# A two-layer hybrid trunk on one core: the first quarter of the first MLP matrix becomes seven block products

## The chip, the cores and the metric

The kernel runs on one core of one Trainium2 chip. The metric is the device time of one execution in microseconds. Three runs of the kernel before the change took 1278.21, 1278.3 and 1280.88 us, so its median is 1278.3 us. One more execution was profiled.

## The reference

Two layers. Each normalises its input, runs a mixer (windowed attention beside an mLSTM, gated and projected), and then a squared-ReLU MLP. The change touches the MLP alone:

```
for layer in range(2):
    x = mixer(x, ...)
    u = relu(rmsnorm(x, norm_ffn) @ w_ff1)      # x: 512 tokens x 1024, w_ff1: 1024 x 4096
    x = x + (u * u) @ w_ff2                     # w_ff2: 4096 x 1024
```

All values are float32. `setup_inputs` draws normal inputs and weights and scales five of the small gains.

## The kernel before, in words

**Three products for one.** TensorE is fed float32r operands. For the precision of float32, each operand is split into a high part (ScalarE copies it to float32r, L1212) and a low part (VectorE subtracts the high part from the original, L1213); `mm3` then issues high x high, high x low and low x high (L47). So each weight block of 128 partitions x 1024 costs one ScalarE and one VectorE operation before TensorE may use it. The weights' parts lie in a pool of four buffers each (`spl`).

**Quarters.** `mlp` (one call per layer) cuts the 4096 hidden columns into four quarters of 1024. The first matrix makes a quarter of u, feature-major; the second matrix adds that quarter's contribution to the tokens in `xtok`. A quarter of either matrix is a product of 2 x 2 blocks: the first matrix has blocks of 512 inputs by 512 columns, against two halves of the inputs (rows j = 0, 1) and two halves of 256 tokens.

**Seven block products.** `first_slots` (for quarters 1 to 3 before the change) and `second_slots` (for all four) compute the 2 x 2 block product with seven block products, numbered 1 to 7, instead of eight, from sums and differences of blocks. A product of the first matrix is called fQ.n here, one of the second pQ.n, with Q the quarter. Each is a `Slot` of two halves: `prep` loads and splits the weights of a half, `run` issues its matmuls, `done` reads the result from PSUM, and `acts_` prepares the second matrix's other operand (`u_split`). fQ.n has 48 matmuls of 256 columns, pQ.n 24 matmuls of 512 columns.

Sums of weight blocks are made by transfers from GpSimd's queue that accumulate (`more`, L1382 and L1560) or by VectorE (`plus`, L1249). Sums of the normalised inputs (t1 to t4) are made once per layer by VectorE in `t_steps`; each is then split by `two_parts`. For the results, `first_read` copies a product from PSUM, `then_read` (L1478 to L1480) adds a second one to it by VectorE and runs ReLU and square on ScalarE, and `only_read` does ReLU and square straight from PSUM.

**The first quarter before the change** is not done so. `First` computes 256 of its columns with 8 x 2 x 3 matmuls of 512 columns. Two of them run at once, step by step over the eight input tiles, in the order 4 to 7 and then 0 to 3. While they do the first four, the input tiles 0 to 3 are still being finished: the steps in `late` transpose each (L52), split it (L180, L181) and sum its squares (L262), and `factor` makes the row factors. Two further `First` follow as slots.

**The order of the work.** The list `slots` writes the order on TensorE by hand:

```
f01 (two First together), First 2, First 3,
p0.1 f1.1 p0.2 f1.2 p0.5 f1.5 p0.6 f1.6 p0.3 f1.7 p0.7 f1.4 p0.4 f1.3,
(the same for quarters 1/2 and 2/3, the last one ending ... p2.7 f3.4 p2.4 f3.3),
p3.1 p3.5 p3.2 p3.6 p3.3 p3.7 p3.4
```

When half i starts, `go` first issues the weights of all halves up to i + 3, then the operand of the next slot, then the matmuls of half i; at the end of a slot `done`, then what `extra` holds for that half (t1 to t4). Each engine runs its instructions strictly in the order that the framework's scheduler gives them; `high_priority` moves splits, sums and PSUM reads forward in it. Weight loads go out on SP's queue (`ask`, L1239) into eleven buffers (`raw`) that lie on memory of the mixer; the first four loads of an MLP are chained in their order, the others are not.

**A dependency that counts below.** p3.5's operand is u(1,1) - u(1,0) of quarter 3, and u(1,0) is finished by product 3 of the first matrix (f3.3). So f3.3's read, ReLU, square, the difference, and its two parts lie between f3.3 and p3.5.

Of the kernel before, what the change touches and what calls it, by code (L numbers as in the profile page):

```python
# [33 lines left out]
def hybrid_kernel(ctx, tc, x, norm_mix, w_in, att_q_norm, att_k_norm, att_sinks, m_gate_bias,  # L34
# [53 lines left out]
    def banks(which):  # L88

        return now["psum"].tile([P, 2, T], F32, tag=which, name=nm("mm"))  # L90
# [1095 lines left out]
    def mlp(l, norm, late, phase):  # L1186
# [87 lines left out]
        class First:  # L1274


            def __init__(self, q, which="f"):
                self.q, self.which, self.w = q, which, {}

            def load(self, h):  # L1280
                with tc.high_priority():
                    r = raw([P, 4, H])
                    ask(r, w_ff1[l, 4 * h * P:4 * (h + 1) * P, H * self.q:H * (self.q + 1)]
                        .rearrange("(k p) n -> p k n", p=P))
                self.w[h] = w_split(r)
                drop(r)

            def step(self, k, order=range(KT)):
                if k == order[0]:
                    self.ps = banks(self.which)  # L1290
                hi, lo = self.w[k // 4]
                for m in range(2):
                    c = slice(m * P, (m + 1) * P)
                    mm3(self.ps[:, m, :], hi[:, k % 4, c], lo[:, k % 4, c], acts[k][0], acts[k][1],
                        k == order[0], k == order[-1])

            def evac(self, u):
                i, m = self.q // 2, 2 * (self.q % 2)
                with tc.high_priority():
                    for t in range(2):  # L1300
                        dst = u[t, i][:, m:m + 2, :]
                        sc.activation(dst, self.ps[:, :, H * t:H * (t + 1)], AF.Relu)
                        sc.activation(dst, dst, AF.Square)

# [5 lines left out]

        def first_slot(q, u, which):
            f = First(q, which)
            return Slot(f.load, lambda h: [f.step(k) for k in range(4 * h, 4 * h + 4)], lambda: f.evac(u))

# [10 lines left out]
        def t_steps():  # L1325

            (h11, l11), (h12, l12), (h21, l21), (h22, l22) = ([f32(a) for a in quad(j, t)]
                                                              for j in range(2) for t in range(2))

            def b12():  # L1330
                scratch["a"] = raw([P, 4, H])
                ve.tensor_tensor(scratch["a"], h12, l12, op=ALU.add)

            def t1():
                d = scratch["b"] = raw([P, 4, H])
                ve.tensor_tensor(d, h11, scratch["a"], op=ALU.subtract)
                ve.tensor_tensor(d, d, l11, op=ALU.add)
                t_parts[1] = two_parts(d, *t_new("t1"))

            def t2():  # L1340
                d = scratch["b"]
                ve.scalar_tensor_tensor(d, d, -1.0, h22, op0=ALU.mult, op1=ALU.subtract)
                ve.tensor_tensor(d, d, l22, op=ALU.subtract)
                t_parts[2] = two_parts(d, *t_new("t2"))

            def t3():

                d = scratch["a"]
                ve.tensor_tensor(d, h22, d, op=ALU.subtract)
                ve.tensor_tensor(d, d, l22, op=ALU.add)  # L1350
                t_parts[3] = two_parts(d, *quad(0, 1))
                drop(d)

            def t4():
                d = scratch["b"]
                ve.scalar_tensor_tensor(d, d, -1.0, h21, op0=ALU.mult, op1=ALU.subtract)
                ve.tensor_tensor(d, d, l21, op=ALU.subtract)
                t_parts[4] = two_parts(d, *t_new("t4"))
                drop(d)

            return [b12, t1, t2, t3, t4]

        def first_slots(part, new):
# [20 lines left out]
            def w2(h):  # L1384
                load(a12, h, 0, 1)
                return a12[h], lambda: None, a12[h]

            def w1(h):
                load(a11, h, 0, 0)

                def then():
                    load(s, h, 1, 0)
                    more(s, h, 1, 1)

                return a11[h], then, a11[h]
# [18 lines left out]
            def w4(h):  # L1414
                load(a22, h, 1, 1)
                return a22[h], lambda: None, a22[h]

            def fresh_y():
                ys[:] = [aux(), aux()]
# [3 lines left out]
            def product_(y, fresh, w, moving, done):  # L1423
# [9 lines left out]
                def run(h):  # L1433
                    if h == 0 and fresh:
                        if y:
                            fresh_y()
                        else:
                            pairs["f"] = banks("f")
# [55 lines left out]
            return {  # L1494
                1: product_(False, True, w1, lambda: quad(0, 0), done1),
                2: product_(True, not seeded, w2, lambda: quad(1, 0), done2),
                5: product_(True, True, w5, lambda: t_parts[1], lambda: first_read((1, 1), True, -1.0)),
                6: product_(False, False, w6, lambda: t_parts[2], lambda: first_read((1, 0), False)),
                7: product_(False, False, w7, lambda: t_parts[3], lambda: then_read((1, 1), False, ALU.subtract)),
                4: product_(False, False, w4, lambda: t_parts[4], lambda: only_read((0, 1), False, -1.0)),  # L1500
                3: product_(True, False, w3, lambda: quad(1, 1), lambda: then_read((1, 0), True, ALU.add)),
# [41 lines left out]
        def second_slots(part, u):  # L1543
# [28 lines left out]
            def w1(h):  # L1572
# [4 lines left out]
                load(qa, h, 0, 0)  # L1577
                load(b12, h, 0, 1)
# [33 lines left out]
            def s4():  # L1612
# [26 lines left out]
        f01, turned = [First(0, "f"), First(1, "y")], [4, 5, 6, 7, 0, 1, 2, 3]  # L1639
        for h in (1, 0):  # L1640
            for f in f01:
                f.load(h)
        weave([(0.5, lambda k=k, f=f: f.step(k, turned)) for k in turned for f in f01], late + [(4.5, factor)])
        for f in f01:
            f.evac(us[0])
        slots = [first_slot(2, us[0], "x"), first_slot(3, us[0], "f")]
        for part in range(4):
            p = second_slots(part, us[part])
            if part < 3:
                f = first_slots(part + 1, us[part + 1])  # L1650
# [99 lines left out]
```

## Time and profile before

| | |
|---|---|
| median of three runs | 1278.3 us (1278.21 to 1280.88) |
| profiled execution | 1280.18 us, span 1278.5 us |
| mean granted TensorE clock over the span | 0.999 |
| first matmul of the MLP, first and second layer | 317.8 and 953.5 us |
| HBM read | 188.95 MB |

The span runs from the first to the last instruction on the core; all times inside an execution are counted from its start. An engine's row gives when an instruction began and how long it took; matmuls overlap, so the pace of TensorE is the distance from one start to the next, not a matmul's own duration. A bracket behind a row is the time for which the engine had stood idle and what ended it. In the waits, the three numbers are the total in us, how often, and the longest.

### The profile page before, as it was taken

The numbers are of one execution on the slowest core, as the hardware profiler recorded it, in microseconds if no ns is written. First come the engines' busy times: TensorE is split into PE (matmuls) and PEld (weight loads), VectorE is DVE, ScalarE is ACT, GpSimd is POOL, SyncE is SP. The second block draws the span as 40 slices with busy tenths as digits, with TensorE's granted clock in tenths as the row PEclk, the third lists the DMA queues.
The fourth block names the chain that finished last, engine by engine and source line by source line (L and its number), as shares of the span: only waits on it lengthen the run. The fifth ranks groups of instructions, "written<-read, shape, count | busy, mean of one in ns | idle before, by whom it ended". The sixth has DMA issues, their size and how long they took to land.

```text
span 1278.5 us, 19222 instructions
## 1 busy us (share of the span) xinstructions
PE 1266.4 (99%) x6882; PEld 1090.9 (85%) x6882; DVE 1011.8 (79%) x1604; ACT 795.5 (62%) x1415; POOL 265.5 (21%) x361
## 2 busy tenths in 40 slices
PE   9999999999999999999999999999999999999998
PEld 7887888888889999998888888788888899999987
DVE  4788988688777787877857989876878777869787
ACT  5578578546565665656454885776466556566563
POOL 4514131030003031131115132310300030311300
PEclk9999999999999999999999999999999999999999
DMA  5425463476679789897224345534857798997953
GB/s 158 112 76 148 110 121 100 138 146 150 185 198 187 209 179 219 211 182 189 35 76 115 99 116 117 114 111 130 157 134 201 192 183 230 168 231 179 206 140 99
DMA packets 138928, 193.35 MB, mean 151 GB/s; under 512 B 10568, under 2 KB 79024, under 8 KB 138832
## 3 DMA queue, kind: packets, MB, share of 16 engines
q1 hardware_dynamic: 92992, 129.72, 33.1%
q0 software_dynamic: 45120, 62.00, 30.2%
q8 instruction: 54, 0.88, 0.3%
q10 hardware_dynamic: 720, 0.40, 0.1%
q14 instruction: 42, 0.34, 0.1%
HBM read 188.95 MB, written 2.10 MB: 149 GB/s over the span
## 4 chain that ended last, share of the span: by engine, by line
PE 88%; DVE 6%; ACT 3%; DMA 1%; POOL 1%; issue 1%; SPq 0%; DVEq 0%; ACTq 0%; POOLq 0%
PE mm L47 74%; PE aux L47 12%; PE aux L52 2%; DMA w<-in_w_in_dram 1%; ACT t L664 1%; DVE wl L168 1%; DVE wl L1213 1%; ACT wh L167 0%; DVE p L748 0%; DVE t L304 0%; DVE tq L625 0%; DMA w<-in_w_m_branch_dram 0%; POOL rp L547 0%; POOL rq L548 0%; DVE m L658 0%
## 5 line engine op out<-in xcount | busy, mean ns | idle before, releaser
L47 PE MATMUL mm<-i,wh 128*128 128x512 f32 (+1 forms) x1280 | 353.2, 363 | 0.0
L1213 DVE TENSOR_TENSOR wl<-raw,wh 128x1024 fp32r<-128x1024 f32 x212 | 257.1, 1222 | 116.1 <-ACT wh L1212 111.4
L1212 ACT ACTIVATE wh<-raw 128x1024 fp32r<-128x1024 f32 x212 | 222.8, 1054 | 172.6 <-PE mm L47 99.7
L47 PEld LDWEIGHTS mm<-i,wh 128*128 128x128 f32 x1280 | 221.8, 189 | 29.5
L47 PE MATMUL mm<-i,wl 128*128 128x512 f32 (+1 forms) x640 | 229.2, 359 | 0.0
L47 PE MATMUL mm<-wh,ul 128*128 128x512 f32 x440 | 172.1, 391 | 3.2 <-DVE ul L1213 3.2
L47 PE MATMUL mm<-wh,uh 128*128 128x512 f32 x440 | 172.7, 393 | 0.9 <-ACT uh L1212 0.9
L47 PE MATMUL mm<-wl,uh 128*128 128x512 f32 x440 | 172.3, 392 | 0.0
L1382 POOL DMA_DIRECT2D raw<-in_w_ff_dram x48 | 61.9, 1311 | 413.3 <-DVE wl L1213 222.9
L47 PEld LDWEIGHTS mm<-i,wl 128*128 128x128 f32 x640 | 120.9, 189 | 18.6
L167 ACT ACTIVATE wh<-w 128x512 fp32r<-128x512 f32 (+1 forms) x144 | 86.4, 603 | 61.6 <-PE mm L47 41.9
L168 DVE TENSOR_TENSOR wl<-w,wh 128x512 fp32r<-128x512 f32 (+1 forms) x144 | 96.4, 672 | 35.5 <-ACT wh L167 33.1
L47 PEld LDWEIGHTS mm<-wh,ul 128*128 128x128 f32 x440 | 83.0, 189 | 21.7 <-DVE ul L1213 4.0
L47 PE MATMUL mm<-wh,i 128*128 128x512 f32 (+1 forms) x352 | 99.8, 357 | 1.0 <-ACT wh L167 1.0
L47 PEld LDWEIGHTS mm<-wh,uh 128*128 128x128 f32 x440 | 83.1, 189 | 17.6 <-ACT uh L1212 1.7
L47 PEld LDWEIGHTS mm<-wl,uh 128*128 128x128 f32 x440 | 83.2, 189 | 15.7
L1267 DVE SCALAR_TENSOR_TENSOR x<-mm,ms,x 128x512 f32<-128x512 f32 x98 | 68.9, 745 | 10.7 <-PE mm L47 10.7
L1560 POOL DMA_DIRECT2D raw<-in_w_ff_dram x36 | 43.6, 1212 | 133.6 <-DVE wl L1213 100.9
L47 PEld LDWEIGHTS mm<-wh,i 128*128 128x128 f32 x352 | 62.0, 188 | 10.2 <-ACT wh L167 1.6
L47 PE MATMUL aux<-i,wh 128*128 128x256 f32 x384 | 69.5, 283 | 0.0
L47 PE MATMUL mm<-t,wh 128*128 128x256 f32 x384 | 69.5, 283 | 0.0
L47 PE MATMUL mm<-wl,i 128*128 128x512 f32 (+1 forms) x176 | 62.0, 352 | 0.2 <-DVE wl L168 0.2
(327 smaller groups left out, 2525.5 us busy)
## 6 DMA issues: line engine op xcount, KB each, us to landing
raw<-in_w_ff_dram SPq DMA_DIRECT2D x144, 512.0 KB, 5.1
raw<-in_w_ff_dram POOLq DMA_DIRECT2D x84, 512.0 KB, 8.5
w<-in_w_in_dram SPq DMA_DIRECT2D x112, 256.0 KB, 2.7
a<-in_w_in_dram POOLq DMA_DIRECT2D x32, 256.0 KB, 5.7
qa<-in_w_out_dram POOLq DMA_DIRECT2D x12, 512.0 KB, 5.8
a<-in_w_in_dram SPq DMA_DIRECT2D x16, 256.0 KB, 4.7
w<-in_w_att_branch_dram SPq DMA_DIRECT2D x16, 256.0 KB, 2.9
w<-in_w_m_branch_dram SPq DMA_DIRECT2D x16, 256.0 KB, 2.9
```

The lines of the kernel that those rows point to most:

```text
L47: latest[0] = nc.tensor.matmul(*args, **kw)
L52: latest[0] = nc.tensor.transpose(*args)
L167: sc.activation(wh[:, :off], raw[:, :off], AF.Copy)
L168: ve.tensor_tensor(wl[:, :off], raw[:, :off], f32(wh[:, :off]), op=ALU.subtract)
L664: sc.activation(s3[:, i, :], s3[:, i, :], AF.Exp, bias=m[:, i:i + 1], accum_out=den[:, i:i + 1])
L1212: sc.activation(hi, src, AF.Copy)
L1213: ve.tensor_tensor(lo, src, f32(hi), op=ALU.subtract)
L1267: ve.scalar_tensor_tensor(xh[:, cc], ps[i][:, cc], ms[j][:, b:b + 1], xh[:, cc], op0=ALU.mult, op1=ALU.add)
L1382: gp.dma_start(to[h], src(h, i, j), accum_op=ALU.add)
L1560: gp.dma_start(to[h], src(h, i, j), accum_op=ALU.add)
```

## The change

The class `First` and its slots are gone. Quarter 0 of the first matrix becomes f0.1 to f0.7, made by `first_slots(0, ...)`, for both layers. TensorE's order becomes

```
f0.2 f1.2 f0.1 f0.5 p0.1 f0.6 f0.7 f0.4 f0.3
f1.1 p0.5 f1.5 p0.6 f1.6 p0.3 f1.7 p0.7 f1.3 p0.4 f1.4 p0.2,
p1.1 f2.1 p1.2 f2.2 p1.5 f2.5 p1.6 f2.6 p1.3 f2.7 p1.7 f2.3 p1.4 f2.4,
(the same with quarters 2 and 3, ending ... p2.7 f3.3 p2.4 f3.4),
p3.1 p3.5 p3.2 p3.6 p3.3 p3.7 p3.4
```

so that products 3 and 4 of the first matrix have changed places everywhere. f0.2 and f1.2 use only inputs 4 to 7; the late inputs 0 to 3 are transposed and split between their halves. While a late input tile stands in PSUM, ScalarE also copies it whole (`turn_whole`, two copies of 128x256 per tile); t1, t2 and t3 are then made from the whole copies instead of from high and low parts. For quarter 0 the second block column of weights is summed by VectorE (`begin`) and then extended by accumulating transfers; p0.1's result is added to the tokens by itself (two operations of L1267) instead of being copied into p0.2's banks; and the weights of p0.5 are summed by a transfer instead of VectorE. The lines that carry this:

```diff
+        def turn_whole(k):
+            ps = norm.transposes(k)
+            norm.turn(k, ps)
+            if not whole:
+                whole[:] = [uspl.tile([P, 4, H], F32, tag="uh", name=nm("x")) for _ in range(2)]
+            for t in range(2):
+                sc.activation(whole[t][:, k, :], ps[:, H * t:H * (t + 1)], AF.Copy, scale=norm.gain(k))
+        def x22():
+            h22, l22 = [f32(a) for a in quad(1, 1)]
+            scratch["a"] = uspl.tile([P, 4, H], F32, tag="ul", name=nm("x"))
+            plus(scratch["a"], h22, l22)
+        def t1():
+            d = scratch["b"] = raw([P, 4, H])
+            plus(d, whole[0], whole[1], ALU.subtract)
+            with tc.high_priority():
                 t_parts[1] = two_parts(d, *t_new("t1"))
+        def t2():
+            d = scratch["b"]
+            neither(d, d, scratch["a"])
+            t_parts[2] = two_parts(d, *t_new("t2"))
+        def t3():
+            d = scratch["a"]
+            plus(d, d, whole[1], ALU.subtract)
+            t_parts[3] = two_parts(d, *quad(0, 1))
...
+            if part == 0:
+                def begin(h):
+                    load(c, h, 1, 0)
+                    load(s, h, 1, 1)
+                    plus(s[h], s[h], c[h])
+                    more(c, h, 0, 0)
+                def w2(h):
+                    load(a12, h, 0, 1)
+                    return a12[h], lambda: None, a12[h]
+                def w5(h):
+                    return s[h], lambda: more(s, h, 0, 0)
...
-                done1, done2 = lambda: first_read((0, 0), False), lambda: then_read((0, 0), True, ALU.add)
+                done1, done2 = lambda: then_read((0, 0), False, ALU.add), lambda: first_read((0, 0), True)
...
                 load(qa, h, 0, 0)
+                if part == 0:
+                    return qa[h], lambda: more(qa, h, 0, 1)
                 load(b12, h, 0, 1)
                 return qa[h], lambda: plus(qa[h], qa[h], b12[h]), b12[h]
...
+            alone = part == 0
-                1: product("x", True, w1, lambda: u[0, 0], [], "f" if end else "y"),
-                2: product("f" if end else "y", False, w2, lambda: u[0, 1], [(0, 0, end)]),
+                1: product("x", True, w1, lambda: u[0, 0], [(0, 0, False)] * alone,
+                           None if alone else "f" if end else "y"),
+                2: product("f" if end else "y", alone, w2, lambda: u[0, 1], [(0, 0, end)]),
...
+        begin0, f0 = first_slots(0, us[0], {2: "y", 5: "y"}, [lambda h: f1s[0](h)])
+        begin1, f1 = first_slots(1, us[1], {2: "x"}, [begin0])
+        slots = [f0[2], f1[2], f0[1], f0[5], p[1], f0[6], f0[7], f0[4], f0[3],
+                 f1[1], p[5], f1[5], p[6], f1[6], p[3], f1[7], p[7], f1[3], p[4], f1[4], p[2]]
+        for part in range(1, 4):
...
-                slots += [p[1], f[1], p[2], f[2], p[5], f[5], p[6], f[6], p[3], f[7], p[7], f[4], p[4], f[3]]
+                slots += [p[1], f[1], p[2], f[2], p[5], f[5], p[6], f[6], p[3], f[7], p[7], f[3], p[4], f[4]]
...
-        extra = dict(zip((1, 3, 7, 11, 15), t_steps()))
+        extra = {0: x22, 3: t1, 6: t2, 8: t3, 10: t4}
...
-        weave(steps, side)
+        weave([(1.0, go) for _, go in steps[:5]], norm.steps(0, 1.0, 0.5, turn_whole) + [(4.0, factor)])
+        weave(steps[5:], side)
```

More of the change, by code (lines that the diff above doesn't have):

```diff
@@ L1184, in mixer, with mlp @@
         return norm
-    def mlp(l, norm, late, phase):
+    def mlp(l, norm, phase):
         final = l == DEPTH - 1
@@ L1271, in gain @@
                                 out[0, b * P:(b + 1) * P, j * T + c[0]:j * T + c[1]], xh[:, cc])
[L1274 to L1303, printed above, removed]
         class Slot:
@@ L1323, in t_new @@
             return [comb.tile([P, 4, H], F32R, tag=f"{n}{p}", name=nm(n)) for p in "hl"]
[L1325 to L1337, printed above, removed]
-                t_parts[1] = two_parts(d, *t_new("t1"))
[L1340 to L1361, printed above, removed]
@@ L1363, in first_slots @@
-        def first_slots(part, new):
+        whole = []
+        def turn_whole(k):
[9 more added lines that the diff above has]
+            plus(scratch["a"], h22, l22)
@@ L1369, in first_slots, with t4 @@
+        def t4():
+            h21, l21 = [f32(a) for a in quad(1, 0)]
+            d = scratch["b"]
+            neither(d, d, h21)
+            plus(d, d, l21, ALU.subtract)
+            t_parts[4] = two_parts(d, *t_new("t4"))
+            drop(d)
+        def first_slots(part, new, places={}, begins=()):
             a11, a12, a22, s, c = ([None] * 2 for _ in range(5))
@@ L1385, in w2 @@
                 load(a12, h, 0, 1)
-                return a12[h], lambda: None, a12[h]
+                return a12[h], lambda: [f(h) for f in begins], a12[h]
+            def begin(h):
+                load(s, h, 1, 0)
+                more(s, h, 1, 1)
             def w1(h):
                 load(a11, h, 0, 0)
[L1391 to L1395, printed above, removed]
+                return a11[h], lambda: begin(h) if part > 1 else None, a11[h]
             def w5(h):
```

47 lines of the change are left out of this document (19 added, 28 removed).

## The prediction

> **What bounds the kernel.** First the page's busy times, then the waits of TensorE over the whole span.
>
> ```profile
> PE 1266.4 (99%) x6882; PEld 1090.9 (85%) x6882; DVE 1011.8 (79%) x1604; ACT 795.5 (62%) x1415; POOL 265.5 (21%) x361
> ```
>
> ```profile
> PE mm L47 <- DVE ul L1213: 3.2, 2, 1.6
> ...
> PE mm L47 <- ACT uh L1212: 0.9, 2, 0.4
> ```
>
> TensorE never rests for long, so the time changes only by the number and pace of its matmuls and by its few waits. The two rows are one wait at one place in each layer: for the parts of a second-matrix operand. The timeline of TensorE shows the place in the first layer.
>
> ```profile
> 598.14 0.28 PE L47 MATMUL aux<-i,wl 128*128 128x256 f32 x1
> ...
> 603.50 0.39 PE L47 MATMUL mm<-wh,ul 128*128 128x512 f32 x1
> 604.32 0.50 PE L47 MATMUL mm<-wh,uh 128*128 128x512 f32 x1 [0.43 <-ACT uh L1212]
> 604.65 0.40 PE L47 MATMUL mm<-wl,uh 128*128 128x512 f32 x1
> 606.63 0.67 PE L47 MATMUL mm<-wh,ul 128*128 128x512 f32 x1 [1.58 <-DVE ul L1213]
> ...
> 610.38 0.40 PE L47 MATMUL mm<-wh,ul 128*128 128x512 f32 x1
> ```
>
> 598.14 is the last matmul of f3.3, 603.50 the last of p3.1, 604.32 the first of p3.5. Then the clock: the column before the last two.
>
> ```profile
> 606.60:610.00 3.40, 3.37 (x8) 2.69 (x9) 3.38 (x3) 0.55 (x2) 0.00 (x0) 0.53 0.00 0
> ...
> 1243.00:1247.00 4.00, 4.00 (x20) 3.28 (x19) 3.65 (x4) 1.06 (x1) 0.00 (x0) 1.00 0.00 0
> ```
>
> After the wait of the first layer the granted clock was 0.53 and 3.4 us held only eight matmuls. After the equal wait of the second layer it stayed at 1.00.
>
> **Term 1, the matmuls.** The groups of the plain quarter (317.7 to 362.6 us), and the paces of a 512-column and a 256-column stream:
>
> ```profile
> L47 PE MATMUL mm<-i,wh 128*128 128x512 f32 x128 | 39.9, 393 | 0.0
> L47 PE MATMUL mm<-i,wl 128*128 128x512 f32 x64 | 25.0, 390 | 0.0
> ```
>
> ```profile
> 330.71 0.62 PE L47 MATMUL mm<-i,wh 128*128 128x512 f32 x2
> 331.16 0.39 PE L47 MATMUL mm<-i,wl 128*128 128x512 f32 x1
> 331.39 0.62 PE L47 MATMUL mm<-i,wh 128*128 128x512 f32 x2
> ```
>
> ```profile
> 369.18 0.40 PE L47 MATMUL mm<-i,wh 128*128 128x256 f32 x2
> 369.42 0.28 PE L47 MATMUL mm<-i,wl 128*128 128x256 f32 x1
> 369.54 0.40 PE L47 MATMUL mm<-i,wh 128*128 128x256 f32 x2
> ```
>
> Three matmuls take 0.68 us at 512 columns (0.227 each) and 0.36 us at 256 (0.12 each). The quarter now takes 192 x 0.227 = 43.5 us; seven products of 48 take 336 x 0.12 = 40.3 us. Saved 3.2 us a layer, **6.4 us** in all. An eighth less arithmetic gives only a fourteenth less time, since half a matmul costs more than half. The sixteen transposes stay. The Trainium skill ("TensorE: Matmul & The Clock Gate", Back-to-back issue gap) gives an isolated gap of N/2.4 + 2.5 ns, that is 216 and 109 ns; by it the saving would be an estimated 4.7 us a layer and the forecast below 1267.0. The measured paces, 227 and 120 ns, differ from it and decide.
>
> **Term 2, products 3 and 4 swapped.** From the rows of the timeline: 603.50 to 604.32 is 0.59 us over the pace, 604.32 to 604.65 is 0.11, 604.65 to 606.63 is 1.75, together 2.45 us in each layer; the eight slow matmuls cost another 3.40 - 8 x 0.227 = 1.6 us in the first layer. So 4.1 and 2.45 us. How the wait arises is on VectorE and ScalarE:
>
> ```profile
> 598.96 0.68 DVE L1478 TENSOR_TENSOR u<-u,aux 128x512 f32<-128x512 f32 x1
> ...
> 601.95 1.22 DVE L1249 TENSOR_TENSOR s<-u,u 128x1024 f32<-128x1024 f32 x1
> 603.08 1.22 DVE L1213 TENSOR_TENSOR wl<-raw,wh 128x1024 fp32r<-128x1024 f32 x1
> 604.22 1.22 DVE L1249 TENSOR_TENSOR u<-u,u 128x1024 f32<-128x1024 f32 x1
> 605.36 1.22 DVE L1213 TENSOR_TENSOR ul<-s,uh 128x1024 fp32r<-128x1024 f32 x1
> ```
>
> ```profile
> 599.67 1.06 ACT L1479 ACTIVATE u<-u 128x1024 f32<-128x1024 f32 x1 [0.27 <-DVE u L1478]
> 600.76 1.06 ACT L1480 ACTIVATE u<-u 128x1024 f32<-128x1024 f32 x1
> ...
> 603.20 1.06 ACT L1212 ACTIVATE uh<-s 128x1024 fp32r<-128x1024 f32 x1 [0.43 <-DVE s L1249]
> ```
>
> From f3.3's last matmul (ends 598.42) follow: sum, ReLU, square, difference, high part, ready at 604.26: 5.84 us. Only p3.1, 24 x 0.227 = 5.44 us, covers it. The low part is later still, for a weight split and the sum "u<-u,u" of the next slot run before it. With f3.3 moved in front of p2.4 and f3.4, the cover is p2.4, f3.4 and p3.1: 5.44 + 5.76 + 5.44 = 16.6 us for a chain that ended at 606.58, 8.2 us long. The wait goes: **6.5 us**. Late next there would be f3.4, whose result goes straight through ReLU and square into p3.2 with p3.1 and p3.5 as cover, 10.9 us against 1.06 x 3 + 1.22 = 4.4: nothing.
>
> **Term 3, the same chain anew.** In the new order f0.3, f1.1, p0.5 stand in a row. The chain is the one above (f0.3 finishes u(1,0), p0.5 needs the difference), its cover f1.1, 48 x 0.12 = 5.76 us instead of 5.44. p0.6's sum "u<-u,u" stands two slots behind p0.5 here, not one, so I take it out of the way; the weight split stays. High part 5.84 us after f0.3's end against about 5.6 due: 0.25. Low part one split end later, 1.2 us behind the high one, where 0.45 is free (it serves the third matmul): 0.75. So **1.0 us a layer, +2.0**; from 0 (a chain without its queueing: 0.68 + 1.06 + 1.06 + 1.22 + 1.06 = 5.1 us) to 4.1 (as before, with a slow clock).
>
> **Term 4, p0.1 behind f0.1.** Only f0.5 (5.76 us) lies between. Sum 1.22, ReLU, square and high part 1.06 each make 4.4 us, with the 0.75 us of queueing that the chain above had 5.2: in time. Low part 1.22 later, 6.4, against 5.6 + 0.45: 0.35 us a layer, **+0.7**; from 0 to 1.5 (one more split of 1.06 on ScalarE in front).
>
> **Term 5, the crowded start.** Until f0.6 begins (four products of 5.76 and one of 5.44 from 317.8: 346.3 us) ScalarE and VectorE must do much more than now. Now, VectorE's busy time being the fourth number and ScalarE's the fifth:
>
> ```profile
> 315.60:329.30 13.70, 13.70 (x69) 11.16 (x68) 9.16 (x11) 7.34 (x12) 1.30 (x1) 1.00 0.58 192
> 329.30:346.30 17.00, 17.00 (x76) 14.08 (x76) 13.87 (x18) 11.45 (x22) 0.00 (x0) 1.00 0.59 156
> ```
>
> ```profile
> L644 ACT ACTIVATE t<-aux 128x256 f32<-128x256 f32 x24 | 9.0, 376 | 3.2 <-PE aux L47 2.9
> ```
>
> Together 23.0 and 18.8 of 30.7 us. Then, VectorE: 11 weight splits, two weight sums, x22, two operations each for t1 and t2, f0.1's sum, one low part of u: 20 x 1.22 = 24.4, and four input splits and two sums of 128x512, about 0.7 each by the 0.68 row: 28.6 us. ScalarE: 11 + 2 + 2 + 1 = 16 of 1.06, some 14 of 128x512 (inputs, squares, copies of f0.2, f1.2, f0.5) at an estimated 0.6 between the 0.376 and 1.06 rows, eight whole copies at 0.376: 28.4 us. Both are 93% full, and fit. The tight step is t1: the last transposes come after half 2 (326.4 + 0.6), high part and whole copies 0.6 + 0.75, difference, high and low part 1.22 + 1.06 + 1.22: 331.9 at the earliest, due at 335.1 for f0.5. 3.2 us of slack in queues that are full: I take 0.5 us a layer, **+1.0**; from 0 to 3 a layer (four squares and a split in front).
>
> **What costs nothing.** Of 512 KB transfers, quarter 0 has 16 instead of 8 for the first matrix, and for the second an accumulating one in place of each of two loads: eight more a layer, in a stretch where the DMA share is 0.58 and 0.59. Six accumulations more are behind GpSimd's queue, which has one instruction in these 30 us. p0.1's two additions to the tokens (L1267) have f0.6 as cover; two copies by ScalarE go.
>
> **Sum.** -6.4 - 6.5 + 2.0 + 0.7 + 1.0 = -9.2 us against the profiled execution's 1280.18: 1271.0. The median is 1.9 lower. If its runs lack the 1.6 us of slow clock, it falls by 7.6 to 1270.7, otherwise by 9.2 to 1269.1. I forecast **1270.0**. About 0.2% (2.6 us) is what a measurement can tell from no change.
>
> **Rivals.**
> - *No new wait* (terms 3 to 5 at nothing): -12.9 against the profiled run, 1265.4 to 1267.0. For it: VectorE and ScalarE have idle time in every stretch. Against: chains of 5 us behind covers of 5.76.
> - *The old wait only moves* to p0.5: 2.45 us and a slow clock in both layers, 4.1 instead of 1.0: +6.2, 1276.2, no change that can be told. For: the chain is the same five steps. Against: 0.32 us more cover, and the sum "u<-u,u" further behind. The Trainium skill ("TensorE: Matmul & The Clock Gate", Part 1: The HAM clock gate) halves the clock after an idle window of about 3.4 us; by that alone these 2.45 us would leave the clock, and this case would be 1273.0. The row with 0.53 speaks against it, the row with 1.00 for it.
> - *The start is over-full*: t1 comes 3 us late in each layer: +5, 1275.0.
> - *Slower: a weight load that comes late.* f0.2 and f1.2 use up four loads in 11.5 us, where the plain steps lived on two for their first half, and only the first four loads are chained; the fourth is now one for the weight sum. f1.2's second half (due 326.4, landing by 324.1) may stand among the later ones, and VectorE's weight sum, with all behind it, waits for its load as well. How late that can be, SP's queue shows:
>
> ```profile
> L1239 SPq DMA_DIRECT2D raw<-in_w_ff_dram x4: 440/476/516, 323.0 to 324.6; - x4
> ...
> DMA to landing us min/median/max: 8.4/11.6/13.7
> ```
>
> Issued there, it lands near 335.4: 11.3 us late, with the slow clock 12.9 a layer, 1270.0 + 25.8 = 1296. The kernel is slower once the load is over 5.5 us late in each layer. Against: the buffers are free before.
>
> **Chances.** Forecast (1268 to 1273) 0.52; no new wait 0.18; over-full start 0.12; old wait moved 0.10; late load 0.08. Faster: the first two and most of the third, 0.79; the same 0.13; slower 0.08. The range 1265.5 to 1276.2 leaves out the late load and an edge of the best case.
>
> **What the next profile would show.** No wait at p3.5 and no slow clock there (else term 2 is wrong). 256-column matmuls at 0.12 in quarter 0. A wait for uh or ul at p0.5 of about 1 us and a shorter one at p0.1. f0.5 waiting for t1 or not settles term 5; a wait on wh or wl behind a transfer in f1.2 or f0.1 would be the late load. The forecast is wrong if quarter 0's stretch up to p0.2 isn't shorter than before.

## The result and the profile after

The changed kernel takes 1309.89 us (median of four runs, 1309.07 to 1313.38), the kernel before 1278.26 us beside it. The ratio is 1.0248, with an interval of 1.0225 to 1.0272: slower by 32 us, where 1270.0 had been forecast. The profiled execution took 1310.44 us with a span of 1308.7.

The page of the changed kernel, busy times, and TensorE's waits (total, times, longest):

```profile
PE 1268.4 (97%) x7170; PEld 1106.3 (85%) x7170; DVE 1027.8 (79%) x1620; ACT 818.1 (63%) x1435; POOL 289.2 (22%) x377
```

```profile
PE mm L47 <- ACT wh L1212: 23.9, 6, 9.3
PE mm L47 <- ACT u L1445: 3.9, 2, 1.9
...
PE aux L47 <- DVE wl L1213: 1.7, 2, 0.9
```

The busy time of TensorE is 2 us above the time before (slow matmuls count longer), and its share has fallen from 99 to 97%: the loss is waiting. The wait for ul and uh at p3.5 is gone, and these three are new. In the first row, 9.3 and 8.5 us (one for each layer) stand before f1.2's second half, and 2.7 and 3.2 us at f0.6, which waits for its weights too. TensorE's timeline shows it from its side:

```profile
328.13 0.62 PE L52 MATMUL aux<-ident,x 128*128 128x128 f32 x4
338.07 0.80 PE L47 MATMUL mm<-i,wh 128*128 128x256 f32 x2 [9.31 <-ACT wh L1212]
...
372.21 0.28 PE L47 MATMUL mm<-t,wl 128*128 128x256 f32 x1
374.43 0.51 PE L47 MATMUL mm<-i,wh 128*128 128x256 f32 x2 [1.94 <-ACT u L1445]
```

Up to the transposes of 328.13 TensorE works at its usual pace; then it stands for 9.3 us. 374.43 is the first matmul of f0.7, and 372.21 the last of f0.6. ScalarE names what was missing:

```profile
336.96 2.00 ACT L1212 ACTIVATE wh<-raw 128x1024 fp32r<-128x1024 f32 x2 [4.03 <-DMA raw<-in_w_ff_dram]
...
372.41 1.06 ACT L1212 ACTIVATE wh<-raw 128x1024 fp32r<-128x1024 f32 x1 [1.82 <-PE mm L47]
373.37 1.01 ACT L1445 ACTIVATE u<-mm 128x1024 f32<-128x1024 f32 x1
```

At 336.96 the split of f1.2's second half begins, the moment its weights have landed. SP's queue, in a window around it:

```profile
L1239 SPq DMA_DIRECT2D raw<-in_w_ff_dram x6: 367/484/897, 322.2 to 325.2; - x6
...
DMA to landing us min/median/max: 3.6/8.4/13.0
```

Six loads go out in a bunch at 322.2 to 325.2, f1.2's among them, although its buffer had been free for long. The code asks for it as the sixth load; the scheduler, which is bound to the code's order for the first four alone, put it twelfth on SP. Ahead of it stand loads whose buffers are still in use: the seventh, one of p0.1's, waits for the buffer of the first split and goes out at 317.6, and the eighth, one of f0.4's, for the buffer of f1.2's own first half and goes out at 322.2. The free load stands behind these two: it goes out at 324.6. Then it takes 12.3 us to land, where the first of the six took 3.6: with the bunch under way the DMA share is 0.98 (325 to 337).

After such a gap the clock is low. The windows of the changed kernel (the column before the last two is the clock, the next the DMA share):

```profile
338.00:341.00 3.00, 2.78 (x11) 2.49 (x12) 2.95 (x3) 3.00 (x5) 0.05 (x1) 0.50 0.17 28
...
328.50:346.30 17.80, 8.34 (x50) 7.80 (x49) 10.56 (x12) 11.83 (x23) 2.57 (x2) 0.71 0.80 198
```

In 17.8 us TensorE was busy for 8.3, at a mean clock of 0.71. Neither VectorE nor ScalarE is near full in that stretch (10.6 and 11.8 of 17.8): they wait too.

### The profile page after: what moved, and what is told of

The parts are those of the page before. It is cut to its first block, busy times and chain, and to the rows that moved or that the text cites. A ratio compares the mean times of both kernels' runs of the same rounds, so it can differ in the third digit from the quotient of the medians.

```text
span 1308.7 us, 19864 instructions
## 1 busy us (share of the span) xinstructions
PE 1268.4 (97%) x7170; PEld 1106.3 (85%) x7170; DVE 1027.8 (79%) x1620; ACT 818.1 (63%) x1435; POOL 289.2 (22%) x377
## 3 DMA queue, kind: packets, MB, share of 16 engines
q0 software_dynamic: 52544, 70.39, 33.6%
q1 hardware_dynamic: 94016, 129.72, 32.5%
## 4 chain that ended last, share of the span: by engine, by line
PE 82%; DVE 6%; DMA 4%; ACT 3%; issue 2%; POOL 1%; SPq 0%; DVEq 0%; ACTq 0%; POOLq 0%
PE mm L47 70%; PE aux L47 11%; DMA raw<-in_w_ff_dram 4%; DVE wl L1213 2%; PE aux L52 2%; ACT t L664 1%; ACT wh L1212 1%; DMA w<-in_w_in_dram 1%; DVE wl L168 1%; DVE tq L625 0%; DVE p L748 0%; SPq L1239 0%; ACT u L1445 0%; POOL rp L547 0%; POOL rq L548 0%
## 5 line engine op out<-in xcount | busy, mean ns | idle before, releaser
L1213 DVE TENSOR_TENSOR wl<-raw,wh 128x1024 fp32r<-128x1024 f32 x224 | 270.9, 1220 | 118.5 <-ACT wh L1212 117.5
L47 PE MATMUL mm<-i,wh 128*128 128x256 f32 (+1 forms) x1344 | 336.8, 342 | 22.0 <-ACT wh L1212 18.1
L1212 ACT ACTIVATE wh<-raw 128x1024 fp32r<-128x1024 f32 x224 | 235.0, 1054 | 179.1 <-PE mm L47 88.7
L47 PEld LDWEIGHTS mm<-i,wh 128*128 128x128 f32 x1344 | 227.5, 193 | 43.0 <-ACT wh L1212 19.1
L47 PE MATMUL mm<-i,wl 128*128 128x256 f32 (+1 forms) x672 | 225.7, 337 | 0.0
L1348 POOL DMA_DIRECT2D raw<-in_w_ff_dram x60 | 77.5, 1315 | 407.0 <-DVE wl L1213 114.8
L47 PEld LDWEIGHTS mm<-i,wl 128*128 128x128 f32 x672 | 129.0, 192 | 13.4
L47 PE MATMUL mm<-t,wh 128*128 128x256 f32 x576 | 106.6, 287 | 5.9 <-ACT wh L1212 5.9
L47 PEld LDWEIGHTS mm<-t,wh 128*128 128x128 f32 x576 | 92.2, 195 | 7.7 <-ACT wh L1212 6.3
L47 PE MATMUL mm<-t,wl 128*128 128x256 f32 x288 | 82.6, 287 | 1.5 <-DVE wl L1213 1.5
L1540 POOL DMA_DIRECT2D raw<-in_w_ff_dram x40 | 50.4, 1341 | 149.1 <-DVE wl L1213 98.9
L1267 DVE SCALAR_TENSOR_TENSOR x<-mm,ms,x 128x512 f32<-128x512 f32 x102 | 72.3, 744 | 8.7 <-PE mm L47 8.4
```

The costliest lines, as they stand in the source:

```text
L47: latest[0] = nc.tensor.matmul(*args, **kw)
L1212: sc.activation(hi, src, AF.Copy)
L1213: ve.tensor_tensor(lo, src, f32(hi), op=ALU.subtract)
L1267: ve.scalar_tensor_tensor(xh[:, cc], ps[i][:, cc], ms[j][:, b:b + 1], xh[:, cc], op0=ALU.mult, op1=ALU.add)
L1348: gp.dma_start(to[h], src(h, i, j), accum_op=ALU.add)
L1540: gp.dma_start(to[h], src(h, i, j), accum_op=ALU.add)
```

## The experiments

Theory when they began: the late load costs the most, and behind it f0.7's wait for ScalarE's read of f0.6's banks. Rival: the start is over-full (the sums, whole copies and extra splits), and the load is only where this shows. The kernel before, measured beside each group, had medians of 1277.65 to 1278.08 us.

| run | us | ratio to before, interval |
|---|---|---|
| exchange alone (x1) | 1271.16 | 0.9951 (0.9931 to 0.9970) |
| exchange, eight loads chained (x10) | 1271.10 | 0.9948 (0.9928 to 0.9968) |
| change, ten loads chained (x2) | 1284.96 | 1.0055 (1.0040 to 1.0071) |
| change, six loads chained (x6) | 1297.29 | 1.0170 (1.0144 to 1.0197) |
| x2, f's banks read one by one (x3) | 1288.51 | 1.0083 (1.0068 to 1.0098) |
| x2, late inputs first (x4) | 1289.54 | 1.0100 (1.0076 to 1.0124) |
| x4 and x3's reads, with priority (x5) | 1288.38 | 1.0086 (1.0071 to 1.0101) |
| x2 without operand sums (x7) | 1289.55 | 1.0093 (1.0071 to 1.0116) |
| x2, f0.7 on other banks (x8) | 1276.48 | 0.9988 (0.9975 to 1.0001) |
| x7 and x8 together (x9) | 1281.26 | 1.0028 (1.0015 to 1.0040) |
| x2, p0.1 between f0.6 and f0.7 (x11) | 1292.38 | 1.0114 (1.0099 to 1.0130) |
| x11, t2 earlier (x12) | 1292.68 | 1.0116 (1.0094 to 1.0138) |
| x11, t1 ahead of one weight split (x13) | 1291.66 | 1.0107 (1.0092 to 1.0122) |
| x13, late inputs first (x14) | 1295.82 | 1.0139 (1.0120 to 1.0159) |
| x11, all operands ahead of two weight splits (x15) | 1283.59 | 1.0041 (1.0025 to 1.0057) |
| x15, late inputs first (x16) | 1287.13 | 1.0066 (1.0051 to 1.0081) |

### The exchange alone, and more loads chained where none is late

x1 is the kernel before with only products 3 and 4 of the first matrix exchanged; x10 is x1 with eight loads chained instead of four.

```diff
-                slots += [... p[3], f[7], p[7], f[4], p[4], f[3]]
+                slots += [... p[3], f[7], p[7], f[3], p[4], f[4]]
```

> The kernel before, with products 3 and 4 of the first matrix exchanged in quarters 1 to 3 and nothing else. Theory (the wait at p3.5 is the chain behind f3.3): the wait of 2.45 us in each layer and the slow clock behind it go, 4.9 to 6.5 us: 1271.8 to 1273.4 us. Rival (the wait only moves, to p2.4 or p3.2): within 2 us of 1278.3.

> The kernel before, with products 3 and 4 exchanged and its first eight weight loads chained instead of four. Theory (the order of loads costs nothing as long as TensorE doesn't wait for one; with the plain quarter it didn't): within 1 us of 1271.2. Rival (an ordered queue brings something by itself, also where no wait of TensorE shows it): 3 us or more below 1271.2.

x1 is 6.7 us faster than the kernel before. The place of the former wait, in windows of x1:

```profile
606.00:610.00 4.00, 4.00 (x19) 3.30 (x19) 3.40 (x4) 2.61 (x4) 1.10 (x1) 1.00 0.00 0
```

Nineteen matmuls in 4.0 us, one in 0.21 us, and the clock is 1.00, where the kernel before had nine in 3.4 us at 0.53. Term 2 (6.5 us) holds. x10 is the same within its interval: an order for the loads is neither good nor bad where TensorE waits for none. x1 and x10 are also the only versions that beat the kernel before clearly.

### The late load

x2 chains the first ten loads of an MLP, x6 the first six, in the changed kernel.

```diff
-            if len(first_asked) < 4:
+            if len(first_asked) < 10:
```

> The changed kernel, with the first ten weight loads of each MLP issued in their written order instead of the first four. Theory (the load of f1.2's second half stands behind loads that wait for buffers): the waits of 9.6 and 8.7 us in f1.2 and the slow clock behind them go, 20 us at least; if the waits for the block sums in f0.6 (3.0 and 3.5 us) come from the same lateness, up to 28: 1282 to 1290 us. Rival (ScalarE and VectorE are over-full at the start): the order of loads changes little, 1305 us or more, with waits of 5 us and more left in f1.2, f0.1 or f0.5.

> The changed kernel with the first six loads chained instead of four or ten: f1.2's second half is then the sixth, and the loads of the weight sum's second half and of f0.1 are free to stand behind loads that wait for buffers. Theory (it is that one load that costs the 9.6 us; the others have slack): the wait in f1.2 goes, and the time is within 4 us of 1285.0. Rival (any of the early loads costs as much): a wait of 4 us or more appears at f0.1, f0.5 or behind the weight sum, 1293 us or more.

x2 is 24.9 us faster than the change, 12.5 a layer; the gap at f1.2 is gone. In x6 it is gone too, but f0.1 now waits for its weights. Waits of x6:

```profile
PE mm L47 <- ACT wh L1212: 12.0, 4, 6.1
```

So the rival was right in x6: the loss is the order of the early loads as a whole. The chain of four, which the change left as it was, was one that the former start could live with. x2 is still 7 us slower than before. TensorE in x2:

```profile
330.75 0.28 PE L47 MATMUL mm<-i,wl 128*128 128x256 f32 x1
332.95 0.38 PE L47 MATMUL mm<-i,wh 128*128 128x256 f32 x1 [1.92 <-ACT i L180]
333.74 0.39 PE L47 MATMUL mm<-i,wh 128*128 128x256 f32 x1 [0.40 <-DVE i L181]
...
356.57 0.28 PE L47 MATMUL mm<-t,wl 128*128 128x256 f32 x1
358.80 0.50 PE L47 MATMUL mm<-i,wh 128*128 128x256 f32 x2 [1.94 <-ACT u L1445]
...
387.03 0.40 PE L47 MATMUL aux<-t,wh 128*128 128x256 f32 x2
388.30 0.39 PE L47 MATMUL aux<-t,wl 128*128 128x256 f32 x1 [0.87 <-DVE wl L1213]
```

Three places: f0.1 waits for the last late input (2.20 and 0.79 us from start to start, 2.75 over the pace), f0.7 for the read of f0.6 (2.2), and behind p0.5's first matmuls f1.5 waits for a weight's low part (1.0 over the pace). All three come in both layers. ScalarE in x2 shows how the first two arise:

```profile
329.93 1.06 ACT L1212 ACTIVATE wh<-raw 128x1024 fp32r<-128x1024 f32 x1 [0.69 <-PE mm L47]
330.89 1.06 ACT L1445 ACTIVATE u<-mm 128x512 f32<-128x512 f32 x2
331.85 0.48 ACT L1298 ACTIVATE x<-aux,gcol 128x256 f32<-128x256 f32 x1
332.20 0.70 ACT L180 ACTIVATE i<-aux,gcol 128x512 fp32r<-128x512 f32 x1
...
356.77 1.06 ACT L1212 ACTIVATE wh<-raw 128x1024 fp32r<-128x1024 f32 x1 [1.82 <-PE mm L47]
357.74 1.01 ACT L1445 ACTIVATE u<-mm 128x1024 f32<-128x1024 f32 x1
```

The high part for which f0.1 waits (332.20) stands behind a weight split that had to wait for TensorE to free a buffer (0.69), the copies of f1.2's result, and a whole copy. The read at 357.74 could have begun when f0.6 ended; another weight split that waited for the same moment was put before it.

### The read of f0.6's banks

x3 reads f0.6's result in two pieces, so that f0.7 could begin on the first bank; x8 gives f0.7 banks of its own and leaves out the addition of products 1 and 6 to it.

```diff
-                if not y:
-                    return [(q, pairs["f"]...)]
-                return [(q[:, 2 * h:2 * h + 2, :], ys[h]...) for h in range(2)]
+                two = ys if y else one_each(pairs["f"])
+                return [(q[:, 2 * h:2 * h + 2, :], two[h]...) for h in range(2)]
```

```diff
-                7: product_(7, False, False, w7, ..., lambda: then_read((1, 1), False, ALU.subtract)),
+                7: product_(7, part == 0, part == 0, w7, ..., lambda: then_read((1, 1), part == 0, ALU.subtract)),
```

> As the kernel with ten chained loads, and a product that fills the banks f is read from PSUM bank by bank, so that its first half can be read while its second half runs. Theory (f0.7 follows f0.6 at once and adds onto the banks that ScalarE is still copying: the 2.2 us between them): those 2.2 us go in each layer, 4.4 us less than the kernel with ten chained loads alone. Rival (f0.7 waits for its own operand t3): the 2.2 us stay, within 1 us of it.

> The kernel with ten chained loads, with f0.7 on two other PSUM banks, so that it needn't wait for the read of f0.6; f0.7 then leaves out the addition of products 1 and 6. Theory (f0.7 adds onto banks that ScalarE is still reading): the 2.1 us between f0.6 and f0.7 go in each layer and the slow clock behind them too, 4 to 7 us less than 1285.0. Rival (f0.7 waits for t3 or its weights): within 2 us of 1285.0.

x3 is 3.6 us slower than x2: its two reads began at 360.22, behind two weight splits, and the wait grew from 1.9 to 2.7. x8 is 8.5 us faster than x2, and f0.7 follows f0.6 without a gap:

```profile
358.07 0.28 PE L47 MATMUL mm<-t,wl 128*128 128x256 f32 x1
358.19 0.40 PE L47 MATMUL aux<-i,wh 128*128 128x256 f32 x2
358.43 0.28 PE L47 MATMUL aux<-i,wl 128*128 128x256 f32 x1
```

So the wait is the dependency on the banks: f0.7 adds to the PSUM content that ScalarE has yet to copy, and directly behind f0.6 nothing covers the copy. Twice 2.1 us, the slow clock after one of them, and the 1.0 us a layer at f1.5, which x8 lost as well, are most of the 8.5.

### Is the start too full?

x4 gives the split of the late inputs priority, x5 adds this for the reads by bank. x7 leaves out the whole copies and the sums t1 to t4 and multiplies an existing block instead; x9 is x7 with x8's banks.

```diff
-            norm.turn(k, ps)
+            with tc.high_priority():
+                norm.turn(k, ps)
```

> The kernel with ten chained loads, and the splits of the late input tiles (the steps woven into f0.2 to f0.1) moved forward in the queues of ScalarE and VectorE. Theory (f0.1 waits 2.1 + 0.7 us because ScalarE splits weights and copies f1.2 before it splits the last late tile): that wait goes in each layer, 1285.0 less 4 to 6: 1279 to 1281 us. Rival (ScalarE is simply full, and what is moved back comes late in turn): the wait moves to f0.5 or p0.1 and the time stays within 2 us of 1285.0.

> As the one with the late inputs first; besides, f0.6 is read bank by bank and these two reads stand in ScalarE's queue ahead of the weight split that stood there before them. Theory (f0.7 adds onto the banks that f0.6's read still holds, and the wait is the read plus what ScalarE does ahead of it): of the 2.1 us at most 1.3 stay, and the slow clock behind them, 1.6 us in the first layer, goes: 2 to 5 us below the kernel with the late inputs first alone. Rival (reading in two pieces costs more than it brings, as in the third kernel): at or above it.

> The kernel with ten chained loads, without the sums of inputs: the whole copies, x22 and t1 to t4 are left out, and an existing operand block is multiplied in their place, so that TensorE's work stays the same. Per layer ScalarE has 12 operations less and VectorE 12 less, nearly all of them in the first 40 us of the MLP. Theory (the waits of 2.8, 0.6 and 0.5 us at f0.1, f0.5 and p0.1 come from what ScalarE and VectorE must do there in all): those waits go, 7 to 9 us less than 1285.0. Rival (they come from single steps in a bad order, which other work doesn't touch): at least half of the waits stays, less than 4 us.

> Both at once: no sums of inputs, and f0.7 on other banks. If the late loads, the crowded start and the adjacent f0.6 and f0.7 are all that stands against the saved matmuls, about 1 us of waits a layer is left (p0.5), and the time is 6.4 - 2 = 4 us below the kernel with the exchange alone (1271.2): 1265 to 1270 us. If something else costs time, it stays above 1272.

In x4 the wait at f0.1 goes and others stand at f0.5 and f0.6 (TensorE's waits of x4: "t" of VectorE 5.9 us in all, "wh" 3.0). That is what the rival said, but the time did not stay: it rose by 4.6 us. x5 is 1.2 us below x4, less than x4's own spread (1287.44 to 1293.95), and f0.7's wait stays (3.5 us in two times): one weight split still ran ahead of the two reads. x7 speaks against the rival in its plain form: with eight copies, x22 and four sums less there is room, and the wait at f0.1 goes, yet others come at f0.2 and p0.1, and x7 is 4.6 us slower than x2. It is no clean test of fullness, though, since the scheduler orders the remaining work anew. x9, which the theory put at 1265 to 1270, misses by 11. ScalarE and TensorE in x9:

```profile
340.95 1.06 ACT L1456 ACTIVATE u<-u 128x1024 f32<-128x1024 f32 x1
344.94 1.06 ACT L1212 ACTIVATE wh<-raw 128x1024 fp32r<-128x1024 f32 x1 [2.93 <-DMA raw<-in_w_ff_dram]
345.91 1.04 ACT L1212 ACTIVATE uh<-u 128x1024 fp32r<-128x1024 f32 x1
```

```profile
343.74 0.28 PE L47 MATMUL mm<-i,wl 128*128 128x256 f32 x1
347.00 0.80 PE L47 MATMUL mm<-wh,uh 128*128 128x512 f32 x1 [2.98 <-ACT uh L1212]
```

Here ScalarE is not busy: u is squared at 342.0, and its high part, for which p0.1 is to start at 343.7, waits until 345.9, since a weight split that has no weights yet stands ahead of it for 2.9 us. That gave a third theory: what counts is neither the amount of work nor one place, but the order on ScalarE. An operand that is ready stands behind the split of a weight that isn't.

### The order on ScalarE

x11 puts p0.1 between f0.6 and f0.7, which covers the read and leaves nothing out. x12 also makes t2 earlier. x13 is x11 with one weight split, that of f0.6's first half, issued behind t1's high part; on ScalarE's queue t1 moves ahead of it, and some small instructions behind it change places. x15 has both of f0.6's weight splits behind t1, t2 and p0.1's high part; for this it also makes p0.1's operand earlier and prepares the weights of two halves one half later. x14 and x16 add x4's edit to x13 and x15. The edits of x11 and x13:

```diff
-        slots = [f0[2], f1[2], f0[1], f0[5], p[1], f0[6], f0[7], f0[4], f0[3],
+        slots = [f0[2], f1[2], f0[1], f0[5], f0[6], p[1], f0[7], f0[4], f0[3],
```

```diff
                     r, then, *gone = w(h)
-                    ws.append(w_split(r))
+                    with tc.issue_after(t1_high[0].ins) if part == 0 and n == 6 and h == 0 else ExitStack():
+                        ws.append(w_split(r))
```

> The ten loads chained, and the order f0.5, f0.6, p0.1, f0.7 in place of f0.5, p0.1, f0.6, f0.7; nothing is left out. Theory (f0.7 pays because it follows at once on the product whose banks ScalarE still reads): 24 matmuls of 512 columns, 5.4 us, now cover the read, p0.1 has 5.8 us more for its operand, and the 2.2 us gap with its slow clock goes as it did with f0.7 on other banks: 8.5 us less than 1285.0, 1276.5, if nothing else becomes late. Rival (the start is short of time on VectorE and ScalarE): f0.6 begins 5.4 us earlier, its operand t2 is made no earlier, and a wait of 2 us or more for t2 stands at f0.6 in each layer: 1280 to 1285. The profile tells by whether the longest gap is before f0.7 or before f0.6.

> As the run with p0.1 between f0.6 and f0.7, and t2 is made half a product earlier (behind the second half of f0.1), t3 and t4 behind p0.1. Theory of order: t2 is in time, no wait at f0.6 and none at f0.7; what stays is f0.1's wait of some 3 us and p0.5's of 1.1 us in each layer: 1274 to 1277. Rival of the full queues: two operations for t2 stand in front of t1's parts or of a weight split, the wait at f0.5 grows by what f0.6 gains, and the time is that of the other run or above it.

> The run with p0.1 between f0.6 and f0.7, with one more edit: the split of f0.6's first weight half is issued behind t1's high part on ScalarE instead of just ahead of it. In that run this weight split began at 342.20 after 6.15 us of waiting for its transfer, and t1's high part, whose sum ended at 336.70, began at 343.16 right behind it; f0.5 lost 4.03 + 1.45 + 0.38 us and paid for a slow clock after it. Theory (the order on ScalarE, not its fullness, makes the wait): t1's high part begins at about 336.8, f0.5 waits under 0.8 us, and the weights of f0.6, landing at 342.2, are still in time for a product that starts about 345: 6 to 8 us less per layer, 1276 to 1281. Rival (full queues: what is moved behind becomes late): f0.6 waits in f0.5's place, 1286 or more.

> The run before this one, and the splits of the late inputs moved ahead of the weight splits as in the run with late inputs first. Theory of order: f0.1's wait of 2.2 + 0.8 us in each layer goes, and since p0.1 lies between f0.6 and f0.7 there is room behind it: 1270 to 1276. Rival (full): the wait moves to f0.5 or f0.6 as it did there, and the time is that of the run before this one or above.

> The run with p0.1 between f0.6 and f0.7, with both weight splits of f0.6 issued behind t1, f0.1's ReLU and square, t2 and p0.1's high part on ScalarE. Theory (operands stand behind weight splits that wait for their accumulating transfers; ScalarE is not full): no wait at f0.5, none at f0.7; f0.1 keeps its 3.0 us; f0.6's weights, landing at about 342 and 345 in the earlier runs, hold up f0.6 by no more than 2 us in each layer: 1276 to 1282. Rival (full, or the transfers themselves are too slow when f0.6 follows at once on f0.5): f0.6 waits 4 us or more in each layer, 1286 or more; then ScalarE's row tells which, busy in front of the wait (full) or idle for a transfer.

> The run before this one with the splits of the late inputs moved ahead of the weight splits. Theory: f0.1's 3.0 us per layer go too, 1270 to 1277. Rival (transfers too slow): what f0.1 gains f0.6 loses, for its weights' transfer is started by the splits of f0.5's weights and not by the inputs: the same time as the run before this one.

x11: f0.7 follows p0.1 at its pace (365.02 to 365.25), so the covered read costs nothing; but f0.5 waits. Timelines of TensorE and of ScalarE in x11:

```profile
340.22 0.28 PE L47 MATMUL mm<-i,wl 128*128 128x256 f32 x1
344.25 0.39 PE L47 MATMUL mm<-t,wh 128*128 128x256 f32 x1 [3.75 <-ACT t L1212]
...
365.02 0.39 PE L47 MATMUL mm<-wh,ul 128*128 128x512 f32 x1
365.25 0.40 PE L47 MATMUL mm<-i,wh 128*128 128x256 f32 x2
```

```profile
342.20 1.06 ACT L1212 ACTIVATE wh<-raw 128x1024 fp32r<-128x1024 f32 x1 [6.15 <-DMA raw<-in_w_ff_dram]
343.16 1.04 ACT L1212 ACTIVATE t<-raw 128x1024 fp32r<-128x1024 f32 x1
```

ScalarE sat idle for 6.15 us with t1's split, whose sum had ended at 336.70, right behind. What it waited for is on GpSimd's queue in x11:

```profile
331.07 1.28 POOL L1348 DMA_DIRECT2D raw<-in_w_ff_dram  x1 [4.22 <-DVE wl L1213]
```

The weights of f0.6 are those of f0.5 with a block added by a transfer, and this can start only when f0.5's low part has been made: for the first half at 331.07. It lands 11.0 us later, at 342.1, with four plain loads (327.99 to 330.09) under way beside it. In x12 the wait at f0.5 is the same thing (5.5 and 3.6 us from start to start in the two layers, 4.0 and 4.2 in x11), and the time is that of x11, as its rival said. In x11 neither the theory (1276.5) nor the rival as written (a wait for t2) came in: the wait was for t1. In x13 t1 is split at 337.05 and f0.5 has no gap, as the third theory says, but the time is only 0.7 us less. ScalarE in x13:

```profile
337.05 1.06 ACT L1214 ACTIVATE t<-raw 128x1024 fp32r<-128x1024 f32 x1
342.36 1.06 ACT L1214 ACTIVATE wh<-raw 128x1024 fp32r<-128x1024 f32 x1 [4.25 <-PE mm L47]
...
345.00 1.06 ACT L1214 ACTIVATE wh<-raw 128x1024 fp32r<-128x1024 f32 x1 [1.49 <-DMA raw<-in_w_ff_dram]
...
346.06 1.04 ACT L1463 ACTIVATE u<-u 128x1024 f32<-128x1024 f32 x1
```

The next operands are now behind the same two weight splits: p0.1's ReLU (346.06), whose sum on VectorE had ended at 340.6, and t2. TensorE in x13:

```profile
345.03 0.28 PE L47 MATMUL mm<-t,wl 128*128 128x256 f32 x1
350.14 0.80 PE L47 MATMUL mm<-wh,uh 128*128 128x512 f32 x1 [4.82 <-ACT uh L1214]
```

TensorE stood 5.1 us at p0.1, of which the scheduler had put one matmul ahead of f0.6. The rival's number (1286 or more) came in, and its place, the start of f0.6; its reason did not, for ScalarE was idle for 4.25 and 1.49 us there. x14 is the same again, with 8.08 us of idle ScalarE before f0.6's weights and t2 behind. x15, where no operand is behind them, is the first to gain: 8.8 us less than x11. TensorE's timeline in x15, and a window of it:

```profile
344.96 0.50 PE L47 MATMUL mm<-t,wh 128*128 128x256 f32 x2 [0.34 <-ACT wh L1214]
348.05 0.50 PE L47 MATMUL mm<-wh,uh 128*128 128x512 f32 x1 [2.58 <-ACT wh L1214]
```

```profile
339.90:349.00 9.10, 6.18 (x49) 5.73 (x48) 8.96 (x14) 8.45 (x10) 2.23 (x2) 1.00 1.13 181
```

f0.6's own weights come in time within 0.4 us; what is left is one matmul of p0.1 that the scheduler put among f0.6's, and that waits 2.6 us for p0.1's weights, split after f0.6's. In these 9.1 us VectorE is busy for 8.96 and ScalarE for 8.45: here the start is full, and this much of the rival holds. The time, 1283.59, lies above the theory's 1276 to 1282. x16 gives the rival right for the late inputs: f0.1's gain is lost at f0.6, whose weight splits wait 1.0 and 1.6 us for their transfers.

So shown, with ten loads chained: x11's gap at f0.5 comes from ScalarE's order, since x13 removed it by that order, and x13's gap of 5.1 us shrinks the same way to 0.3 and 2.6 us in x15. For x9 the order is read from the trace, and no run tests it. Behind the order stands the transfer that lands late, in a stretch where x11's DMA share is 1.14 (329.0 to 344.2; the share adds up the time of packets and can pass one). Whether fewer transfers there would serve as well as another order, no run tests.

In time the orders brought little. x15 is 1.4 us below x2, less than the two intervals tell apart; none that kept all the work went under 1283.6, and even x8 stays 5.3 us above the exchange alone. Open: whether an order by hand on ScalarE and TensorE could bring the whole change to the 1265 to 1270 us that the matmuls allow.

## Why the prediction was wrong

**The step that failed.** The late load was a rival at 0.08 ("f1.2's second half ... may stand among the later ones"), set aside with "Against: the buffers are free before." That looked at f1.2's own buffer. On SP's queue it counted whether the buffers of all loads ahead were free, and two were not (317.6 and 322.2). So the sum put the late load at nothing, and it cost most of the 40 us between forecast and result: chaining ten loads took away 24.9. The mechanism that the rival named was right. That its price, 25.8 us, came so close is in part luck: the gaps were 9.3 and 8.5 us and not 11.3, the clock was low for longer (0.50 from 338 to 341 and on to 343.3), f0.6 lost 3.5 and 3.9 us to its own weights, which the rival had not named, and chaining brought a new wait at f0.1. The chance was the error, and the order in which the scheduler had put the first dozen loads on SP would have set it right; the code's own order does not show it.

**A wait that was not seen.** Of f0.7 the prediction said nothing. In the old order of products another quarter's product lies between 6 and 7 of the first matrix; in the new one f0.7 adds to banks that ScalarE is still to read. It cost 8.5 us with what hung on it (x8).

**Term 5, a size.** The crowded start was put at 0.5 us a layer (0 to 3) and at t1 before f0.5. Behind the chained loads it is 2.75 us a layer at f0.1, for the last late input's parts, and a slow clock after it in one of the layers (in x8 0.51 in the 3.4 us from 334.4); small gaps make up most of the rest of x8's 6.5 us above the forecast. Whether order or fullness (93% in the count) makes the wait at f0.1 is not settled: the rows show it behind a weight split and copies, but x4 and x16, which took it away, lost as much further on.

**"What costs nothing."** The DMA share was read as 0.58 and 0.59 in the kernel before, with room for eight more transfers. With ten loads chained it is near or above one from the start. The windows of x2:

```profile
317.00:329.00 12.00, 11.97 (x101) 11.77 (x101) 11.24 (x12) 8.46 (x15) 2.58 (x2) 1.00 0.99 253
329.00:345.90 16.90, 13.88 (x107) 12.86 (x107) 13.74 (x15) 15.21 (x25) 5.94 (x6) 1.00 1.11 236
```

An accumulating transfer took 11.0 us there (331.07 to 342.1 in x11), and operands stood behind its split: that is part of what was taken as free. The transfers of the two queues are not equal in cost either. By the page of x2, GpSimd's queue, where the accumulating ones go, moved 70.39 MB with 34.5% of the DMA engines' time and SP's 129.72 MB with 32.7%, about half as much for a byte.

**What held.** Term 1: the matmuls run at the forecast pace; f0.7's start in x8 shows 0.36 us for three of 256 columns (358.07 to 358.43). No run shows the 6.4 us by themselves. Term 2: 6.7 us against 6.5. Term 3 held in its number by luck alone: there is a gap of 1.0 us a layer among p0.5's first matmuls, but it is f1.5 that waits there, for a weight's low part, and not p0.5 for ul. Term 4: p0.1's wait for ul is 0.3 us at most in x2 ("PE mm" on "ul", 0.5 us in two times), as put.

Of the clock, which the prediction weighed at the old wait, these are windows of x2 right after gaps of 2.2 us:

```profile
358.80:362.20 3.40, 3.40 (x17) 3.40 (x18) 1.00 (x2) 0.00 (x0) 0.00 (x0) 0.57 1.18 240
...
998.40:1001.80 3.40, 3.39 (x28) 3.39 (x29) 1.02 (x2) 0.34 (x1) 0.00 (x0) 1.00 1.13 303
971.20:974.60 3.40, 3.40 (x16) 3.40 (x17) 1.23 (x1) 2.08 (x7) 0.01 (x1) 0.50 1.00 278
```

The gap before f0.7 left 0.57 in the first layer and 1.00 in the second; the one before f0.1 left 0.50 in the second, and there the clock stayed low for 6.8 us, until 977.1. The Trainium skill ("TensorE: Matmul & The Clock Gate", Part 1: The HAM clock gate) has the clock fall after at least one idle window of about 3.4 us, and calls the window free-running. The trace agrees that the same gap may or may not be hit, and not that 3.4 us of idling are needed.

## What to carry to other kernels

When a change adds loads to an in-order queue, list the first loads in the order in which the scheduler put them on the queue, which need not be the code's, write the release of each one's buffer beside it, and ask what is behind the first that must wait; a free buffer further back is no help. Do the same on the engine that splits or copies: an operand that is ready can stand behind the split of a weight that a transfer is still adding to, and an engine that is idle by its share can still be what everyone waits for. A product that adds to the banks of the one just before it needs another product between the two.

## What the runs showed of the hardware

ScalarE does not pass over an instruction that waits: in x11 it idled 6.15 us with a ready split behind, which agrees with the Trainium skill ("Perfetto Trace Analysis", Tensor Engine Instruction), where ScalarE's and VectorE's queues are called strictly first in, first out. Gaps of 2.2 us were enough in x2 to halve the TensorE clock in some places, for 3.4 us (from 359.3) and for 6.8 us (from 970.3), and not in others.
